# Conditioning weights in a ring of their own: whole visits, loaded one visit ahead

## The chip, the cores and the metric

The kernel runs on one core of one Trainium2 chip. The metric is the device time of one execution, in microseconds. Names used below: PE is the matrix engine (TensorE), PEld its weight loads, DVE the vector engine, ACT the scalar engine, POOL the third elementwise engine (GpSimd), SP the engine that issues the loads from HBM.

## The reference

One layer of a hybrid decoder, for 256 prompt tokens and 8 x 4 sample tokens (288 rows in all), model width 2048, all weights float32. What matters here:

```
mod = silu(c) @ w_ada + b_ada                  # nine conditioning rows, 2048 -> 6 x 2048
sh1, sc1, g1, sh2, sc2, g2 = split(mod, 6)     # "parts" 0 .. 5
h    = rmsnorm(x, norm1) * (1 + sc1) + sh1
proj = h @ w_in                                # pooled inputs, z gate, conv inputs, dt
mix  = concat(pool_mixer(...), ssd_mixer(...)) @ w_out
x    = x + g1 * mix
h2   = rmsnorm(x, norm2) * (1 + sc2) + sh2
up   = h2 @ w_up;  act = silu(causal_conv(gate)) * val
x    = x + g2 * (act @ w_down)
y    = rmsnorm(x, norm_f)
```

## The kernel before

All activations lie transposed: a tile holds 128 features by 288 rows. Every large product is done with three multiplications of a float32 value split in two (`mm3`, lines 302 to 304: weight high by input high, weight high by input low, weight low by input high). A weight block of 128 x 1024 (512 KB) is loaded into a *raw* slot, ACT casts it to the high half (line 288, `whi`), DVE subtracts to get the low half (line 290, `wlo`), and after that the raw slot is free. Eight PE products of 128 x 128 by three can be made from one block; one output tile of a 2048-long product takes two blocks and 48 matmuls.

The order of the work on PE is: the input projection in seven blocks (`xbc`), in the last of which all 28 tiles run over the last quarter of the input; then eight more tiles of it (`uz`), between which the state-space mixer (`ssd_group`, convolutions, pooling) runs; then the output projection, 16 tiles (`out`); then the second norm, the up projection (`upk`, `gate`, `val`) and the down projection.

The conditioning product `mod` has few rows, so for it the weights are the moving operand: parts 0 and 1 are needed first and are done during the early blocks. Parts 2, 3, 4 and 5 are done by `ada_part_units`: 16 steps over the 2048 inputs, each with two raw blocks (`adap`, 512 KB each) and four matmuls of 512 columns, which use a quarter of the array each (`tile_position`) and run side by side. A step's four matmuls are eight records in the trace. After the 16 steps the sum is copied (`asb`), transposed (`adat`) and added to the bias by DVE (line 419). Between two `yield`s lie AY = 2 steps, that is four blocks and 16 records: this is called a visit. Parts 2, 3 and 4 (the first gate, the second norm's shift and scale) are a chain `adas`, pulled at rates (RA1, RA2, TA, ADA_OUT) through the last `xbc` block, the `uz` tiles and the output projection, and part 5 (`adag2`) later.

```
adas = chain(*(ada_part_units(p, AY) for p in (2, 3, 4)))
...
pull(adas, RA1 / AY)          # each of the 28 tiles of the last xbc block
...
pull(adas, RA2 / AY)          # each eighth of a uz tile
...
pull(adas, TA / AY)           # once, before the output projection
...
pull(adas, (1 + (m >= 14 - ADA_OUT)) / AY)   # after each out tile
```

A scheduler places the instructions of each engine by its own estimate and may part the matmuls of one visit. Raw blocks of all kinds take turns in one ring of slots (class `_W`): 8 in the pool `w1`, 8 more in `w0` until the last `xbc` block, and one in `w2` from the sixth `out` tile on; `whi` and `wlo` have two slots in `w1` and two in `w2`. All these loads, those of the states (`h0`) and of `x` are issued by SP in one order; a load whose slot is not yet free holds up every load behind it.

Of the kernel before, what the change touches and what calls it, by code (L numbers as in the profile page):

```python
# [36 lines left out]
ET = XT + len(UEARLY) + 3 * ZEARLY  # L37
EPS = 1e-6
WU = (14, 2, 2, 2, 6)
RAW0, RAW1, RAW2 = 8, 8, 1  # L40
SPLIT0, SPLIT1, SPLIT2 = 1, 2, 2
YK = 2
AQ = (4, 4, 4, 4, 4, 4)
# [5 lines left out]
TP = 0.4  # L49
TV, TL = 2.0, 2.8  # L50
GB = 4
AY = 2

RA1, RA2, RB1, RB2, RB3 = 0.5, 0.4, 1.0, 1.0, 1.0
TA, ADA_OUT = 4, 4
TK = 4
GA = (2, 3)
XM = (0, 2, 5, 9)
# [105 lines left out]
def kernel(ctx: ExitStack, tc, ins, outs):  # L164
# [98 lines left out]

    wp = [None]

    def load(key):
        off, cols = S.items[key]
        t = wp[0].tile([P, RAWC], F32, tag="raw", name="raw_" + "_".join(map(str, key)))
        nc.sync.dma_start(t[:, :cols], wflat[off:off + P * cols].rearrange("(p n) -> p n", p=P))
        return t  # L270

# [3 lines left out]

    def top_up():

        while queue and nloads[0] - min((n for n, _ in ahead.values()), default=nloads[0]) < RAW0 + RAW1:
            key = queue.popleft()
            ahead[key] = (nloads[0], load(key))  # L280
            nloads[0] += 1
# [69 lines left out]
    def ada_group_units(gi):  # L351
# [49 lines left out]
            nc.vector.tensor_tensor(o, src, b.unsqueeze(3).to_broadcast([P, 2, nj // 2, NC9]), ALU.add)  # L401
        ada_scale(0, 1, early[:, V_N1:V_N1 + KT], k0, gk)

    def ada_part_units(part, ay=1):
        ps = pa.tile([P, 512], F32, tag="ada", name=f"adap{part}")
        for k in range(KT):
            raws = [load(("adap", part, k, h)) for h in range(2)]
            for h in range(2):
                ada_mm(ps, raws[h], k, 0, 512, range(2 * h, 2 * h + 2))
            if k % ay == ay - 1:  # L410
                yield
        asb = ada_sb(ps, 512, f"p{part}")
        yield
        pt = ada_tr(asb, 512, f"p{part}")
        for i in range(4):
            o = ada[:, part].rearrange("p (j i) c -> p j i c", j=4)[:, :, i, :]
            b = bada[:, part].rearrange("p (j i) -> p j i", j=4)[:, :, i]
            src = pt[:, i * P:(i + 1) * P].rearrange("p (j c) -> p j c", j=4)[:, :, 0:NC9]
            nc.vector.tensor_tensor(o, src, b.unsqueeze(2).to_broadcast([P, 4, NC9]), ALU.add)
        if part == 4:  # L420
            ada_scale(1, 4, vec[:, V_N2:V_N2 + KT], 0, KT)
        yield

    def samp(ap):
        return ap.rearrange("p (b l) -> p b l", b=NB)
# [30 lines left out]
    class _W:  # L456


        def __init__(self):
            self.slots = {"raw": [], "whi": [], "wlo": []}  # L460
            self.i = {"raw": 0, "whi": 0, "wlo": 0}

        def add(self, pool, nraw, nsp):
            for tag, n in (("raw", nraw), ("whi", nsp), ("wlo", nsp)):
                m = len(self.slots[tag])
                if m:
                    r = self.i[tag] % m
                    self.slots[tag] = self.slots[tag][r:] + self.slots[tag][:r]
                    self.i[tag] = 0
                self.slots[tag] += [(pool, n)] * n  # L470

        def drop(self, pool):
            for tag, sl in self.slots.items():
                r = self.i[tag] % len(sl)
                self.slots[tag] = [x for x in sl[r:] + sl[:r] if x[0] is not pool]
                self.i[tag] = 0

        def tile(self, shape, dt, tag, name):
            pool, n = self.slots[tag][self.i[tag] % len(self.slots[tag])]
            self.i[tag] += 1  # L480
            return pool.tile(shape, dt, tag=tag, name=name, bufs=n)

    wp[0] = _W()
    wp[0].add(ctx.enter_context(tc.tile_pool(name="w1", bufs=1, side="right")), RAW1, SPLIT1)
    mx_ctx = ExitStack()
    mx = mx_ctx.enter_context(tc.tile_pool(name="mx", bufs=1))
    xa = []
# [10 lines left out]
    w0_ctx = ExitStack()  # L498
    w0 = w0_ctx.enter_context(tc.tile_pool(name="w0", bufs=1))
    shift(w0, 32)  # L500
    wp[0].add(w0, RAW0, SPLIT0)
    sx = [None]

    cvp = [mx.tile([P, 5, CW], F32, tag="cvp", name=f"cvp{g}", bufs=4) for g in range(4)]
# [159 lines left out]
    def drain(gen):  # L664
        for _ in gen:
            pass
# [246 lines left out]
    def chain(*gens):  # L913
        for gn in gens:
            yield from gn

    adas = chain(*(ada_part_units(p, AY) for p in (2, 3, 4)))
    with in_order(*(e.engine for e in (nc.tensor, nc.scalar, nc.vector))):
        nc.scalar.activation(warm, sc_c[:, 0, 0:1], AF.Sqrt, scale=0.0)
        warm_pe(WU[0])  # L920
# [75 lines left out]
    def pull(gn, rate):  # L996

        credit[id(gn)] = credit.get(id(gn), 0.0) + rate
        while credit[id(gn)] >= 1:
            credit[id(gn)] -= 1  # L1000
            next(gn, None)

    nloads[0] = len(first) + KT // 4
    for bi in range(len(BLOCKS)):
        last = bi + 1 == len(BLOCKS)
        top_up()
        if last:

            wp[0].drop(w0)
            w0_ctx.close()  # L1010
            sx[0] = mx_ctx.enter_context(tc.tile_pool(name="sx", bufs=1, reuse_waits="tile"))
            raw = load(("dt",))[:, :KT * NH].rearrange("p (k h) -> p k h", h=NH)
            wdt = wp[0].tile([P, RAWC], F32R, tag="whi", name="whi_dt")
            with tc.high_priority():
                nc.gpsimd.memset(wdt.bitcast(F32), 0.0)
                both = wdt[:, :DTW * KT].rearrange("p (k c) -> p k c", c=DTW)
                nc.scalar.copy(both[:, :, 0:NH], raw)
                nc.vector.tensor_tensor(both[:, :, 32:32 + NH], raw, both[:, :, 0:NH].bitcast(F32), ALU.subtract)
            ps = pm.tile([P, 512], F32, tag="mm", name="mm_dt")
            for k in range(KT):  # L1020
                w = wdt[:, DTW * k:DTW * k + P]
                nc.tensor.matmul(ps[:, :N], w, xhi[0][k], start=k == 0, stop=False)
                nc.tensor.matmul(ps[:, :N], w, xlo[0][k], start=False, stop=k == KT - 1)
            late_states()
            dt_stage(ps)
        elif bi == 4:
            nc.sync.dma_start(vec, ins["vec"])
        elif bi == 5:
            late_loads()
        for i, m in enumerate(xbc_units(bi)):  # L1030
            if not last:
                top_up()
                if bi == 0 and i in (3, 7, 13):
                    ci = {3: 2, 7: 3, 13: 4}[i]
                    ready["xbc", 0, ci] = split(fetch(("xbc", 0, ci)), 0, len(_xbc_chunks(0)[ci][1]) * P,
                                                f"xbc0_{ci}", pin=True)
                if i in VIS[bi]:
                    next(nxt)
                    top_up()
            else:  # L1040
                pull(back, 0.5 if m < 20 else RB1) if m >= 9 else None
                pull(adas, RA1 / AY)

    late = {}
    n = 0
# [1 line left out]
    for m in list(range(4 + 3 * ZEARLY, 16)) + ULATE:  # L1047
        for _ in uz_units(m):
            n += 1
            for gn in late.values():  # L1050
                pull(gn, 0.5)
            pull(adas, RA2 / AY)
            pull(back, RB2 if n <= zlast else RB3)
            if n == zlast:
                drain(back)
                back = chain(ssd3, y_norm())
        if m < 4:
            late[m] = pool_units(m)
            next(late[m])
    pull(adas, TA / AY)  # L1060
    for h, (_, n) in enumerate(_halves(KT)):
        ready[("out", 0, h)] = split(load(("out", 0, h)), 0, n * P, f"out_0_{h}")
    for gn in late.values():
# [68 lines left out]
    for m in range(16):  # L1132
        if m in XM:
            sl = slice(4 * XM.index(m), 4 * XM.index(m) + 4)
            nc.sync.dma_start(x[:, sl, :], ins["x"][:, sl, :])
        if m == 5:
            wp[0].add(w2, RAW2, SPLIT2)
        for i, ps in enumerate(project_units(("out", m), KT, order=MIXK)):
            if m == KT - 1 and i == 5:
                all_but_last("ssum2")  # L1140
        residual(ps, 2, m)
        squares(m, "a")
        pull(adas, (1 + (m >= 14 - ADA_OUT)) / AY)
        if m == 13:
            drain(adas)


    adag2 = ada_part_units(5)
    for k in range(2):
        ready[("upk", k)] = split(load(("upk", k)), 0, 2 * FK * P, f"upk{k}")  # L1150
# [282 lines left out]
```

## Time and profile before

| | us |
|---|---|
| median of 3 runs | 1358.78 |
| lowest, highest | 1358.45, 1361.12 |
| the profiled execution's own time | 1359.14 |
| its span, first to last instruction | 1357.2 |
| PE busy | 1340.9 |
| DVE, ACT, POOL busy | 808.8, 580.3, 223.8 |
| moved by DMA | 323.18 MB |

The profile page gives busy time by engine, then 40 slices of the span, the DMA queues, the chain of work that ended last, and groups of instructions. The other views are asked of the same trace: the waits of an engine, the chain in order of time, a timeline of one engine, and sums over windows of time. A PE record's end is modelled, so the distance from one start to the next is the better price of a matmul.

### The profile page before, as it was taken

The page shows a single profiled execution, that of the slowest core. Times are in us where ns is not written, and L with a number is a line of the kernel's source. Part 1 is how long each engine was busy: PE and PEld are TensorE (multiplying, and loading weights), DVE is VectorE, ACT ScalarE, POOL GpSimd, SP SyncE. Part 2 cuts the span into 40 slices and gives each one's busy share as a digit, 9 for nine tenths or more (in the row PEclk, how much of TensorE's full clock was granted, in tenths as well). Part 3 has the DMA queues.
Part 4 walks back from the last instruction along what each step waited for, and adds up shares of the span by engine and source line. Part 5 has one row for each costly group of instructions (what it writes and reads, how often), then busy time and mean ns, then how long its engine had stood idle before and what let it go on. Part 6 is the DMA issues. An engine that isn't in the chain of part 4 may idle for free.

```text
span 1357.2 us, 26159 instructions
## 1 busy us (share of the span) xinstructions
PE 1340.9 (99%) x10517; PEld 1249.0 (92%) x10517; DVE 808.8 (60%) x1348; ACT 580.3 (43%) x911; POOL 223.8 (16%) x435
## 2 busy tenths in 40 slices
PE   9999999999999999999999999999999999999997
PEld 8889997776779889999999999999999999999997
DVE  5675568778564348645565455656554556566553
ACT  5343244577543335534443334443433334444452
POOL 0000012123121213111211001311220011132221
PEclk9999999999999999999999999999999999999999
DMA  9999768878878878787555555655555555566541
GB/s 371 405 408 365 257 245 320 341 263 296 301 278 321 323 263 261 244 288 272 184 184 184 162 180 183 201 190 184 176 186 167 186 188 192 187 205 191 181 120 70
DMA packets 97481, 323.18 MB, mean 238 GB/s; under 512 B 10768, under 2 KB 19920, under 8 KB 97360
## 3 DMA queue, kind: packets, MB, share of 16 engines
q1 hardware_dynamic: 93600, 310.79, 66.1%
q0 software_dynamic: 3184, 9.69, 2.0%
q8 instruction: 82, 1.34, 0.4%
q10 hardware_dynamic: 576, 1.03, 0.2%
q14 instruction: 39, 0.32, 0.1%
HBM read 309.78 MB, written 10.39 MB: 236 GB/s over the span
## 4 chain that ended last, share of the span: by engine, by line
PE 74%; DVE 1%; issue 0%; POOL 0%; ACT 0%; DVEq 0%; POOLq 0%
PE mm_down L303 7%; PE mm_down L302 7%; PE mm_down L304 7%; PE mm_val L303 6%; PE mm_gate L303 6%; PE mm_gate L302 6%; PE mm_val L304 6%; PE mm_gate L304 6%; PE mm_val L302 6%; PE adap L331 3%; PE mm_out L302 3%; PE mm_out L303 3%; PE mm_out L304 3%; PE mm_up L303 1%; PE mm_up L302 1%; PE mm_up L304 1%
## 5 line engine op out<-in xcount | busy, mean ns | idle before, releaser
L303 PE MATMUL mm_down<-al,whi_down 128*128 128x288 f32 x688 | 202.5, 294 | 0.0
L302 PE MATMUL mm_down<-ah,whi_down 128*128 128x288 f32 x688 | 202.4, 294 | 0.0
L304 PE MATMUL mm_down<-ah,wlo_down 128*128 128x288 f32 x688 | 202.0, 294 | 0.0
L303 PE MATMUL mm_gate<-h2l,whi_gate 128*128 128x288 f32 x640 | 188.8, 295 | 0.0
L303 PE MATMUL mm_val<-h2l,whi_val 128*128 128x288 f32 x640 | 188.8, 295 | 0.0
L304 PE MATMUL mm_val<-h2h,wlo_val 128*128 128x288 f32 x640 | 188.7, 295 | 0.0
L304 PE MATMUL mm_gate<-h2h,wlo_gate 128*128 128x288 f32 x640 | 188.6, 295 | 0.0
L302 PE MATMUL mm_gate<-h2h,whi_gate 128*128 128x288 f32 x640 | 188.5, 294 | 0.0
L302 PE MATMUL mm_val<-h2h,whi_val 128*128 128x288 f32 x640 | 187.7, 293 | 0.0
L290 DVE TENSOR_TENSOR wlo_gate<-raw_gate,whi_gate 128x1024 fp32r<-128x1024 f32 x80 | 98.2, 1229 | 136.5 <-ACT whi_gate L288 136.3
L290 DVE TENSOR_TENSOR wlo_down<-raw_down,whi_down 128x1024 fp32r<-128x1024 f32 x96 | 107.5, 1120 | 116.9 <-ACT whi_down L288 116.9
L288 ACT CAST whi_down<-raw_down 128x1024 fp32r<-128x1024 f32 x96 | 92.5, 964 | 167.0 <-PE mm_down L303 117.8
L288 ACT CAST whi_gate<-raw_gate 128x1024 fp32r<-128x1024 f32 x80 | 84.2, 1054 | 159.7 <-PE mm_gate L303 66.9
L288 ACT CAST whi_val<-raw_val 128x1024 fp32r<-128x1024 f32 x80 | 84.2, 1053 | 120.8 <-issue 101.6
L302 PE MATMUL xbc<-h1h,whi_xbc 128*128 128x288 f32 x448 | 133.4, 301 | 0.8 <-ACT h1h L452 0.7
L303 PE MATMUL xbc<-h1l,whi_xbc 128*128 128x288 f32 x448 | 132.0, 296 | 0.0
L304 PE MATMUL xbc<-h1h,wlo_xbc 128*128 128x288 f32 x448 | 130.0, 295 | 0.0
L302 PEld LDWEIGHTS mm_down<-ah,whi_down 128*128 128x128 f32 x688 | 129.2, 188 | 0.0
L303 PEld LDWEIGHTS mm_down<-al,whi_down 128*128 128x128 f32 x688 | 129.1, 188 | 0.0
L304 PEld LDWEIGHTS mm_down<-ah,wlo_down 128*128 128x128 f32 x688 | 129.0, 188 | 0.0
L302 PEld LDWEIGHTS mm_gate<-h2h,whi_gate 128*128 128x128 f32 x640 | 120.3, 188 | 5.0 <-ACT ah L1198 3.4
L302 PEld LDWEIGHTS mm_val<-h2h,whi_val 128*128 128x128 f32 x640 | 120.3, 188 | 0.0
(325 smaller groups left out, 2983.4 us busy)
## 6 DMA issues: line engine op xcount, KB each, us to landing
raw_adap<-wflat SPq DMA_DIRECT2D x128, 512.0 KB, 6.1
raw_gate<-wflat SPq DMA_DIRECT2D x80, 512.0 KB, 3.5
raw_val<-wflat SPq DMA_DIRECT2D x80, 512.0 KB, 3.9
raw_ada<-wflat SPq DMA_DIRECT2D x64, 512.0 KB, 9.6
raw_xbc<-wflat SPq DMA_DIRECT2D x50, 512.0 KB, 9.1
raw_down<-wflat SPq DMA_DIRECT2D x48, 512.0 KB, 3.6
raw_out<-wflat SPq DMA_DIRECT2D x32, 512.0 KB, 7.4
raw_down<-wflat SPq DMA_DIRECT2D x32, 384.0 KB, 3.1
```

The costliest lines, as they stand in the source:

```text
L288: yield nc.scalar.copy(hi[:, :n], raw[:, a:a + n])
L290: yield hi, lo, nc.vector.tensor_tensor(lo[:, :n], raw[:, a:a + n], hi[:, :n].bitcast(F32), ALU.subtract)
L302: nc.tensor.matmul(ps, whi[:, w], bh, start=first, stop=False)
L303: nc.tensor.matmul(ps, whi[:, w], bl, start=False, stop=False)
L304: nc.tensor.matmul(ps, wlo[:, w], bh, start=False, stop=last)
L331: nc.tensor.matmul(ps[32 * j:32 * j + 32, :nb], sc_c[:, k, :], raw[:, c:c + nb], start=(k == 0), stop=(k == KT - 1), tile_position=(0, 32 ...
```

## The change

Parts 2 and 3 are now done by a new generator, `ada_visits`, in visits of two steps (AK = 2); part 4 in four visits of four steps (AK2 = 4) after the output tiles 2, 5, 8 and 11. A visit's loads are issued one visit ahead, right behind the matmuls of the visit before. Its matmuls take the blocks in reverse order, so that the first one waits for the last load, and are tied to each other (high priority, program order), so that the scheduler keeps them together. The blocks have a ring of their own, `rawa`: four of the eight slots of `w1` go over to it when the last `xbc` block begins, and four more in `w2` join it at the first output tile (RAW2 = 4); at the end of the output projection all eight return to the common ring, which then has 12 slots where it had 9. From the last `xbc` block to the end of the output projection the ring of all other weights has four slots. The two `whi` and `wlo` slots of `w2` join at the first output tile instead of the sixth. VA spreads the 16 visits of parts 2 and 3: five in the last `xbc` block, nine in `uz`, the rest drained before the output projection.

```diff
-RAW0, RAW1, RAW2 = 8, 8, 1
+RAW0, RAW1, RAWA, RAW2 = 8, 4, 4, 4
-AY = 2
-RA1, RA2, RB1, RB2, RB3 = 0.5, 0.4, 1.0, 1.0, 1.0
-TA, ADA_OUT = 4, 4
+VA = (5, 9, 2)
+AK, AK2, AOUT = 2, 4, (2, 5, 8, 11)
...
+    def ada_visits(parts, step):
+        plan = [(part, k0) for part in parts for k0 in range(0, KT, step)]
+        def chunks(v):
+            part, k0 = plan[v]
+            return [(k, h, load(("adap", part, k, h), "rawa")) for k in range(k0, k0 + step) for h in range(2)]
+        ahead, end = chunks(0), None
+        yield
+        for v, (part, k0) in enumerate(plan):
+            if end:
+                ada_end(*end)
+                end = None
+            if k0 == 0:
+                ps = pa.tile([P, 512], F32, tag="ada", name=f"adap{part}")
+            n = 0
+            for k, h, raw in ahead[::-1]:
+                for j in (2 * h, 2 * h + 1):
+                    with tc.high_priority() if n else nullcontext():
+                        i = nc.tensor.matmul(ps[32 * j:32 * j + 32, :], sc_c[:, k, :],
+                                             raw[:, 512 * (j % 2):512 * (j % 2) + 512], start=k == step - 1,
+                                             stop=k == KT - step, tile_position=(0, 32 * j))
+                    tc.keep_in_program_order(i)
+                    n += 1
+            if v + 1 < len(plan):
+                ahead = chunks(v + 1)
+            if k0 + step == KT:
+                end = part, ada_sb(ps, 512, f"p{part}")
+            yield
+        ada_end(*end)
+        yield
...
-    adas = chain(*(ada_part_units(p, AY) for p in (2, 3, 4)))
+    adas = ada_visits((2, 3), AK)
...
             wp[0].drop(w0)
+            wp[0].move("rawa", "raw", "rawa")
...
+            next(adas)
             dt_stage(ps)
...
-                pull(adas, RA1 / AY)
+                pull(adas, VA[0] / 28)
...
-            pull(adas, RA2 / AY)
+            pull(adas, VA[1] / 64)
...
-    pull(adas, TA / AY)
+    drain(adas)
...
-        if m == 5:
-            wp[0].add(w2, RAW2, SPLIT2)
+        if m == 0:
+            for tag, n in (("rawa", RAW2), ("whi", SPLIT2), ("wlo", SPLIT2)):
+                wp[0].add(w2, tag, tag, n)
+            adas = ada_visits((4,), AK2)
+            next(adas)
...
-        pull(adas, (1 + (m >= 14 - ADA_OUT)) / AY)
+        if m in AOUT:
+            next(adas)
         if m == 13:
             drain(adas)
+    wp[0].move("rawa", "rawa", "raw")
     adag2 = ada_part_units(5)
```

More of the change, by code (lines that the diff above doesn't have):

```diff
@@ L51 @@
 GB = 4
-AY = 2
-RA1, RA2, RB1, RB2, RB3 = 0.5, 0.4, 1.0, 1.0, 1.0
-TA, ADA_OUT = 4, 4
+VA = (5, 9, 2)
+AK, AK2, AOUT = 2, 4, (2, 5, 8, 11)
+RB1, RB2, RB3 = 1.0, 1.0, 1.0
 TK = 4
@@ L264, with load @@
     wp = [None]
-    def load(key):
+    def load(key, ring="raw"):
         off, cols = S.items[key]
-        t = wp[0].tile([P, RAWC], F32, tag="raw", name="raw_" + "_".join(map(str, key)))
+        t = wp[0].tile([P, RAWC], F32, tag=ring, name="raw_" + "_".join(map(str, key)))
         nc.sync.dma_start(t[:, :cols], wflat[off:off + P * cols].rearrange("(p n) -> p n", p=P))
@@ L276, in top_up @@
     def top_up():
-        while queue and nloads[0] - min((n for n, _ in ahead.values()), default=nloads[0]) < RAW0 + RAW1:
+        while queue and nloads[0] - min((n for n, _ in ahead.values()), default=nloads[0]) < RAW0 + RAW1 + RAWA:
             key = queue.popleft()
@@ L413, in ada_part_units, with ada_end @@
         yield
+        ada_end(part, asb)
+        yield
+    def ada_end(part, asb):
         pt = ada_tr(asb, 512, f"p{part}")
@@ L421, in ada_part_units @@
             ada_scale(1, 4, vec[:, V_N2:V_N2 + KT], 0, KT)
-        yield
     def samp(ap):
@@ L459, in __init__, with turn, add, move @@
         def __init__(self):
[L460 to L470, printed above, removed]
+            self.slots = {"raw": [], "rawa": [], "whi": [], "wlo": []}
+            self.i = dict.fromkeys(self.slots, 0)
+        def turn(self, ring):
+            sl = self.slots[ring]
+            r = self.i[ring] % len(sl) if sl else 0
+            self.slots[ring], self.i[ring] = sl[r:] + sl[:r], 0
+        def add(self, pool, ring, tag, n):
+            self.turn(ring)
+            self.slots[ring] += [(pool, tag, n)] * n
+        def move(self, tag, a, b):
+            self.turn(a)
+            self.turn(b)
+            self.slots[b] += [x for x in self.slots[a] if x[1] == tag]
+            self.slots[a] = [x for x in self.slots[a] if x[1] != tag]
         def drop(self, pool):
[L473 to L476, printed above, removed]
+            for ring in self.slots:
+                self.turn(ring)
+                self.slots[ring] = [x for x in self.slots[ring] if x[0] is not pool]
         def tile(self, shape, dt, tag, name):
-            pool, n = self.slots[tag][self.i[tag] % len(self.slots[tag])]
-            self.i[tag] += 1
+            pool, tag, n = self.slots[tag][self.ix(tag)]
             return pool.tile(shape, dt, tag=tag, name=name, bufs=n)
+        def ix(self, ring):
+            self.i[ring] += 1
+            return (self.i[ring] - 1) % len(self.slots[ring])
     wp[0] = _W()
-    wp[0].add(ctx.enter_context(tc.tile_pool(name="w1", bufs=1, side="right")), RAW1, SPLIT1)
+    w1 = ctx.enter_context(tc.tile_pool(name="w1", bufs=1, side="right"))
+    for ring, tag, n in (("raw", "raw", RAW1), ("raw", "rawa", RAWA), ("whi", "whi", SPLIT1), ("wlo", "wlo", SPLIT1)):
+        wp[0].add(w1, ring, tag, n)
     mx_ctx = ExitStack()
@@ L500 @@
     shift(w0, 32)
-    wp[0].add(w0, RAW0, SPLIT0)
+    for tag, n in (("raw", RAW0), ("whi", SPLIT0), ("wlo", SPLIT0)):
+        wp[0].add(w0, tag, tag, n)
     sx = [None]
```

## The prediction

> **What bounds the kernel now.** I read the page first, then what PE waited for.
>
> ```profile
> span 1357.2 us, 26159 instructions
> PE 1340.9 (99%) x10517; PEld 1249.0 (92%) x10517; DVE 808.8 (60%) x1348; ACT 580.3 (43%) x911; POOL 223.8 (16%) x435
> ```
>
> ```profile
> PE mm_out L303 <- DVE mixl L1082: 2.0, 1, 2.0
> PE ysum L240 <- POOL ssq L839: 1.2, 1, 1.2
> PE cse L800 <- DVE ada L419: 1.0, 1, 1.0
> ```
>
> PE is busy for 99% of the span. So time can come from two places only: PE work that is not needed, and PE waits, of which the second view (waiter, releaser, total, times, longest) has 4.2 us in the part that changes. Everything else is hidden as long as data is there when PE comes to it. The page has nothing on pieces of visits, so next I read the timeline of PE round a whole visit, the chain round a broken one, and the sum over all of them.
>
> ```profile
> 403.67 0.29 PE L304 MATMUL mm_out<-mixh,wlo_out 128*128 128x288 f32 x1
> 403.90 1.92 PE L331 MATMUL adap<-raw_adap,sc_c 128*32 128x512 f32 x16
> 405.75 0.40 PE L302 MATMUL mm_out<-mixh,whi_out 128*128 128x288 f32 x1
> 405.99 0.29 PE L303 MATMUL mm_out<-mixl,whi_out 128*128 128x288 f32 x1
> ```
>
> ```profile
> 358.56 0.98 PE adap L331 x2
> ...
> 360.50 1.85 PE adap L331 x14
> ```
>
> ```profile
> 196.18:475.00 278.82, 54.71 (x384) 10.70 (x384) 1.18 (x2) 0.99 0.83 306
> ```
>
> A whole visit takes PE from 403.90 to 405.75, 1.85 us. The matmul before it and the one behind it take 0.23 and 0.24 us to the next start; the plain step is 0.134 (405.75 to 418.64 below, 96 matmuls in 12.89). So a visit between full-width matmuls costs another 0.2. In the second view a visit was parted: one matmul (two records) takes 0.98 alone, because its three neighbours do not run beside it, and the rest still takes 1.85: 2.83 instead of 1.85. The third row sums all of parts 2 to 4 (384 records, 24 visits): 54.71 us of PE.
>
> **What the change removes on PE.** 24 whole visits would be busy for 24 x 1.92 = 46.1, so 8.6 is spent on pieces; 0.9 of it lies in half clock, as the piece that starts at 383.40 in the chain shown below, and belongs to the next part, which leaves 7.7. I count 33 runs in the timeline, nine more than visits; a run's record overlaps the next by 0.07 (1.92 against 1.85), so 7.1 is real. In the order in which the changed kernel was built, every visit of parts 2 to 4 stands whole: 16 of 16 records and four of 32.
>
> ```profile
> 501.72 0.76 PE ssum L240 x6
> 502.48 0.97 PE adap L331 x2
> 503.46 0.79 PE pbrstd L253 x6
> 504.24 2.71 PE adap L331 x22
> ```
>
> 24 records (two are missing) take 2.71, so 8 more cost 0.86 and a visit of 32 takes 3.57, 0.13 less than two of 16; four of them 0.5. Between full-width matmuls there are 19 runs now and 11 in the new order: 8 x 0.2 = 1.6. Sum: 7.1 + 0.5 + 1.6 = **9.2 us less**. PE itself hides nothing of it, since it is the bound; what can take it back is a wait.
>
> The 1.0 us wait for DVE's bias addition goes as well: PE stood at a small matmul (`cse`) whose PSUM buffer still held a transposed conditioning sum; in the new order a whole visit, 1.85 us, lies between that transpose and the next `cse`. **1.0 less** (at worst nothing).
>
> **What it moves into a wait: the way into the output projection.** Here PE waits for the gated norm's chain, and this is where the moved visits were filling in.
>
> ```profile
> 364.79 1.42 POOL ssq L839
> ...
> 366.26 0.83 PE ysum L240 x6
> ...
> 370.01 1.13 PE pbrstdy L253 x6
> ...
> 376.11 1.18 DVE wlo_out L290
> ...
> 379.74 0.44 DVE mixl L1082
> ...
> 380.22 0.40 PE mm_out L303
> ...
> 383.40 0.99 PE adap L331
> ```
>
> ```profile
> 364.63:368.05 3.42, 2.22 (x18) 1.99 (x17) 3.39 (x10) 1.91 (x5) 1.42 (x1) 1.00 0.89 307
> 368.05:371.46 3.41, 3.41 (x16) 3.37 (x15) 0.02 (x1) 0.30 (x1) 0.00 (x0) 0.50 0.99 392
> 378.29:381.70 3.41, 1.48 (x8) 1.29 (x9) 3.36 (x13) 2.88 (x8) 0.00 (x0) 1.00 0.98 362
> 381.70:385.11 3.41, 3.41 (x10) 1.54 (x8) 3.41 (x8) 0.44 (x1) 0.47 (x1) 0.50 1.02 418
> ```
>
> The windows (length, busy PE, PEld, DVE, ACT, POOL, then granted clock, DMA share, GB/s) show that each wait here is paid again: after 1.2 and 1.9 us of idle PE in a stretch of 3.41 us the clock is 0.50 for the next 3.41, about 1.7 us lost. The Trainium skill ("TensorE: Matmul & The Clock Gate", section "What's actually happening") grants half the clock after an idle window of about 3.4 us and asks for no gaps above that length; here 1.2 us sufficed, so the trace is harsher than the page.
>
> Now: 1.2 + 1.7 + 2.0 + 1.7 and 0.5 of small change, 7.1 us lost between the last `y` and the end of the third output tile. Changed: between that `y` and `ysum` stand 15 matmuls (2.1 us) instead of 19 and most of a visit; the chain from y to ssq takes about 2.6 by my estimate when ACT is free (1.42 at most for ssq, and three steps of the size of mixl, 0.44), so a wait of 0.5 and no half clock. From `pbrstdy` to the first `mixl` I take 8.6: now 380.2 - 370.0 = 10.2, less one `wlo_out` (1.2), which is done earlier in the new order, and less 0.4 at full clock. PE has only `pbrstdy`, a pool product, three matmuls and one visit in that time, 3.5 us: a wait of 5.1, and half clock behind it, 1.7. Together 7.3 against 7.1. I take **0.2 more** (the visits gone as filler equal the work that is gone; between -2 and +3).
>
> **The third output tile's second half.** This is the new wait.
>
> ```profile
> DMA to landing us min/median/max: 3.3/6.1/13.2
> ```
>
> ```profile
> 405.75:418.64 12.89, 12.89 (x101) 1.00 0.96 371
> 473.11:485.90 12.79, 12.79 (x101) 1.00 1.00 382
> ```
>
> ```profile
> 374.94 1.92 PE L331 MATMUL adap<-raw_adap,sc_c 128*32 128x512 f32 x16
> ```
>
> ```profile
> 375.70 1.05 ACT L288 CAST whi_out<-raw_out 128x1024 fp32r<-128x1024 f32 x1
> ```
>
> ```profile
> 376.03 0.80 SPq L269 DMA_DIRECT2D raw_adap<-wflat  x2
> ```
>
> SP's queue is in order: behind a load that waits for its slot, all that follows waits too. A load takes 3.3 us or more to land, and in a full stretch (the two windows of PE alone above) 382 GB/s are 1.37 us for 512 KB; I use 3.6 for the first and 1.35 for each further one. In the new order SP has, behind the last visit of part 3: two blocks of `adap`, one more, a piece of `x`, another block, a piece of `x`, and only then the second half of output tile 2. The first waits until that visit has given up its first slot, 1.1 us after its start (in the profile SP's next loads follow the visit at 374.94 at 376.03). The seventh lands 1.1 + 3.6 + 6 x 1.35 = 12.8 us after the visit's start, and the cast (1.05) and subtraction (1.18 above) follow. PE has the rest of the visit, 52 matmuls at 0.134 and about 1.2 of small products: 10.1 us. So the first matmul waits 12.8 + 1.1 - 10.1 = 3.8 and the third another 1.0, and 4.8 idle bring half clock for one window: 4.8 + 1.7 = **6.5 more** (between nothing, if SP gets the blocks in earlier, and 9). Who waits behind it: every later output tile, and nothing else.
>
> **The rest of the output projection.** A long visit needs eight blocks: 3.6 + 8 x 1.35 = 14.4 us, and behind them come the next tile's two. The ring of four holds two tiles, 12.9 us; the first blocks are asked for some 2.5 us before the visit ends, as its slots come free. That leaves about 0.5 short at the sixth tile, nothing at the others, where the new order has more of `out` ahead of the eight: **0.5 more** (0 to 7, see the rivals). In `uz` and `xbc` four blocks need 1.1 + 3.6 + 3 x 1.35 = 8.8 us from one visit's start to the next; by the new order the shortest distance is 9.8, so nothing.
>
> **The second norm.** Today one visit lies before `ssum`, a piece of 0.97 behind it and 22 records behind `pbrstd`. In the new order the third column sum stands behind a lone matmul: ssum in two parts with 0.97 between, then eight records (0.99), `pbrstd`, 14 records (1.85), and the modulated input comes about 3.1 after `pbrstd`'s start. 1.85 + 0.55 + 0.97 + 0.4 + 0.99 + 3.1 = 7.9 against 504.24 + 2.71 - (501.72 - 1.85) = 7.1 now: **0.8 more**. In the up and down projections PE waits for nothing now, and twelve slots instead of nine can win nothing there.
>
> **Sum**: -9.2 - 1.0 + 0.2 + 6.5 + 0.5 + 0.8 = -2.2 us against the profiled execution's own 1359.14 (its span 1357.2 and 1.9 round it), that is 1356.9. That execution was 0.4 above the median of the runs, 1358.78; from the median I get 1356.6 and take **1356.7**. No change can be told from one within 0.2%, 1356.1 to 1361.5.
>
> **Rivals.** *The third tile does not wait* (faster). If SP's loads get in earlier, or the 1.0 and half clock fall away, 6.5 goes: 1350.2. For it: SP's order was set by an estimate, and DMA had 0.83 of its time taken from 196 to 475, so there is room. Against it: the slots' order, which no speed of DMA changes.
>
> *Four slots are too few* (slower). If a block takes over 1.35 us, the eight blocks of a long visit and the next tile's (9 x 1.35 + 3.3 = 15.5) outlast two tiles and the lead of 2.5 (15.4). At 1.5 (the median landing of 6.1 shows how far the queue is filled) each of two gaps is 1.7 us late and pays 1.7 at half clock: 6.8 more, 1363.5. For it: 371 GB/s in a normal stretch. Against it: PEclk 1.00 and no wait in the stretch from 405 to 500 today, with the same bytes.
>
> *The clock falls only after a whole idle window*, as the page named above has it. Then 1.7 behind the third tile's wait is not paid: 1355.0. The windows above speak against it, the wait of 1.0 us at `cse`, which cost no clock, a little for it.
>
> **Chances.** Forecast (1354 to 1360) 0.45; third tile free 0.20; four slots too few 0.27; clock 0.08. Faster by over 0.2%: 0.20 + 0.08 + 0.17 of the forecast's 0.45 (what lies below 1356.1) = 0.45; within: 0.28 + 0.05 of the slower case that ends below 1361.5 = 0.33; slower 0.22. The range leaves out the lower half of the faster case and the upper part of the slower one: 1350 to 1364; the likeliest case's own is 1354 to 1360.
>
> **What would show it.** Right: PE time of `adap` up to the end of the output projection about 46 (16 x 1.92 + 4 x 3.64), no run of two records; a wait of `mm_out` for `mixl` near 5 and one for `whi_out` near 4; the clock at 0.50 twice. Wrong: `whi_out` released by DMA at several tiles (four slots), no wait at the third tile, a broken visit, or waits of `adap` for its own blocks.

## The result: 6 us slower, and the profile after

The changed kernel takes 1364.93 us (median of 5 runs, 1364.44 to 1366.04) against 1358.78 before (5 runs, 1358.04 to 1361.12): a ratio of 1.0044, with a 95% interval of 1.003 to 1.0058. The forecast was 1356.7 (1350 to 1364): the wrong side of no change, by 8 us. The profiled execution took 1366.04, with a span of 1364.3, 7.1 more than before.

The page of the changed kernel, first lines:

```profile
span 1364.3 us, 26129 instructions
PE 1336.8 (98%) x10517; PEld 1251.2 (92%) x10517; DVE 813.7 (60%) x1348; ACT 580.4 (43%) x911; POOL 219.7 (16%) x435
```

PE is busy for 4.1 us less, in a span that is 7.1 longer: the work went, and 11 us of idling came. The visits' own PE time in the changed kernel, to be held against the 54.71 of before:

```profile
199.56:480.00 280.44, 46.22 (x384) 10.58 (x384) 0.97 0.83 303
```

It is 8.5 less. With 13 runs of records fewer (33 to 20, at an overlap of 0.07) that is 7.6 of real time, and 7.6 is what the forecast had for pieces and long visits. What PE waited for in the changed kernel (waiter, releaser, total, times, longest):

```profile
PE mm_out L302 <- ACT whi_out L288: 5.2, 2, 4.3
PE mm_out L303 <- DVE mixl L1132: 4.8, 1, 4.8
PE adap L424 <- DMA raw_adap<-wflat: 1.2, 2, 0.6
PE mm_out L304 <- DVE wlo_out L290: 1.1, 2, 0.7
...
PE y L864 <- ACT ec L854: 0.7, 1, 0.7
PE cse L848 <- DVE yo L834: 0.7, 1, 0.7
PE pool L935 <- DVE pout L930: 0.6, 1, 0.6
PE ysum L240 <- POOL ssq L887: 0.4, 1, 0.4
```

Before there were 4.2 us of waits in this part. Here are first three waits of the forecast: `mixl` (4.8, forecast 5.1), the third output tile (4.3 and 0.4, forecast 3.8 and 1.0) and `ysum` (0.4, forecast 0.5). Then come a second wait for `whi_out` at the sixth output tile (0.9, with 0.7 for its low half; forecast 0.5) and a row of waits of 0.5 to 0.7 in the `uz` part, which the forecast did not have. Two of these are a visit waiting for its own blocks (`adap`, 1.2 in all). The clock, in stretches of 3.41 us, the steps in which it changed in these traces (busy PE, PEld, DVE, ACT, POOL, then PEclk, DMA share, GB/s):

```profile
368.25:371.66 3.41, 1.34 (x5) 1.34 (x6) 3.41 (x13) 3.22 (x7) 0.13 (x1) 0.50 1.02 372
371.66:375.08 3.42, 3.42 (x19) 1.83 (x22) 3.42 (x8) 1.38 (x4) 0.00 (x0) 0.50 0.90 367
395.56:398.97 3.41, 0.85 (x2) 0.50 (x2) 1.11 (x1) 1.89 (x2) 0.79 (x1) 0.50 1.03 410
398.97:402.39 3.42, 3.25 (x13) 3.25 (x14) 3.23 (x4) 2.29 (x3) 0.00 (x0) 0.50 0.82 268
422.87:426.28 3.41, 3.41 (x16) 3.41 (x15) 3.41 (x3) 1.81 (x2) 0.16 (x1) 0.50 0.72 191
```

A full-width matmul follows the one before it after 0.24 us at clock 0.50 and after 0.134 at 1.00, so nearly half of the busy time at 0.50 is lost; taken as half it is 2.4, 2.05 and 1.7, together 6.1 us. Before it was 3.4 in two windows. Last, the two places where `whi_out` was late: SP's loads, and the chain back from PE.

```profile
375.65 10.32 SPq L269 DMA_DIRECT2D raw_adap<-wflat  x8
...
387.76 11.69 SPq L269 DMA_DIRECT2D raw_out<-wflat  x5
```

```profile
387.76 9.01 DMA raw_out<-wflat
396.79 1.05 ACT whi_out L288
```

```profile
404.79 4.97 SPq L269 DMA_DIRECT2D raw_adap<-wflat  x8
409.86 16.88 SPq L269 DMA_DIRECT2D raw_out<-wflat  x8
```

```profile
397.86 5.08 DVE L290 TENSOR_TENSOR wlo_out<-raw_out,whi_out 128x1024 fp32r<-128x1024 f32 x4 [3.89 <-ACT whi_out L288]
```

At the third tile the output load goes out at 387.76. Since the output load before it, at 360.65, SP has issued sixteen loads of `adap` and two pieces of `x`; the last four `adap`, from 384.69 on, waited for the last visit's slots. The output load lands 9.0 later, the cast takes 1.05, and PE starts at 397.88. At the sixth tile the eight blocks of one long visit go out at 404.79, the tile's first half behind them at 409.86, and it takes 10.1 to land. From 399.9 to 404.79 SP stood for the visit's first slot. In that time three of the four output slots came free: the four subtractions of the last view end at 399.1, 400.4, 401.7 and 402.9, and only the first slot was taken at once. So here too the output load stood behind the visit's loads in the queue, and not only for want of a slot.

### The profile page after: what moved, and what is told of

Its sections match the earlier page's. It is cut to its first block, busy times and chain, and to the rows that moved or that the text cites. A ratio compares the mean times of both kernels' runs of the same rounds, so it can differ in the third digit from the quotient of the medians.

```text
span 1364.3 us, 26129 instructions
## 1 busy us (share of the span) xinstructions
PE 1336.8 (98%) x10517; PEld 1251.2 (92%) x10517; DVE 813.7 (60%) x1348; ACT 580.4 (43%) x911; POOL 219.7 (16%) x435
## 3 DMA queue, kind: packets, MB, share of 16 engines
q8 instruction: 82, 1.34, 0.4%
## 4 chain that ended last, share of the span: by engine, by line
PE 92%; DMA 4%; DVE 2%; ACT 1%; issue 0%; SPq 0%; POOL 0%; DVEq 0%; POOLq 0%; ACTq 0%
PE mm_down L303 7%; PE mm_down L302 7%; PE mm_down L304 7%; PE mm_val L303 6%; PE mm_gate L303 6%; PE mm_gate L302 6%; PE mm_val L304 6%; PE mm_gate L304 6%; PE mm_val L302 6%; PE xbc L302 5%; PE xbc L303 4%; PE xbc L304 4%; PE adap L424 3%; PE mm_out L304 2%; PE mm_out L303 2%; PE mm_out L302 2%
```

## Experiments

Times are medians of 4 to 12 runs, and each ratio is to the kernel before on the same chip, which took 1358.4 to 1358.9 in all of them.

**Part 4 asked for later, in long visits.**

```
-AK, AK2, AOUT = 2, 4, (2, 5, 8, 11)
+AK, AK2, AOUT = 2, 4, (4, 7, 10, 13)
...
                 wp[0].add(w2, tag, tag, n)
+        if m == 3:
             adas = ada_visits((4,), AK2)
             next(adas)
```

> The changed kernel, but part 4's first eight blocks are asked for ahead of output tile 3 instead of tile 0, and its four visits lie after tiles 4, 7, 10, 13. In the built order the second half of tile 2 is now loaded ahead of them. Theory Q (a place in SP's queue costs the time: the half tile behind part 4's first blocks): the wait at the third tile, 4.7 us, and its half clock, 2.0, go: 1364.9 - 6.7 = 1358.2. Rival S (four slots for the output weights are too few beside eight blocks of conditioning, wherever they stand): the wait comes back at tile 3, 3 to 5 us with half clock behind it: 1363 to 1366.

1361.21, ratio 1.0019 (1.0011 to 1.0028). The wait at the third tile is gone, one of 2.5 and 0.7 is there at the fourth (tile 3 of the code, where S had it), and the half clock behind it did not come in the profiled execution. That execution took 1358.70, 2.5 less than the median; what the others lose was not profiled. The median lies between Q and S: 3.7 of the 6.7 us that Q put on the place in the queue came back.

**Part 4 in short visits.**

```
-AK, AK2, AOUT = 2, 4, (2, 5, 8, 11)
+AK, AK2, AOUT = 2, 2, (2, 4, 5, 7, 8, 10, 11, 13)
```

> The changed kernel, but part 4 in eight visits of two steps (after tiles 2, 4, 5, 7, 8, 10, 11, 13) instead of four of four. In the built order the second half of tile 2 stands ahead of part 4's blocks here too, and no burst is longer than four blocks. Theory Q: the waits at the third tile (6.7 with half clock) and at the sixth (1.7 and 1.7) go, and four more switches and the shorter visits cost 1.3: 1364.9 - 10.1 + 1.3 = 1356.1. Rival S: a wait of 3 to 5 us comes back at tile 3, the sixth tile is free: 1361 to 1363.

1362.65, ratio 1.0027 (1.0018 to 1.0035). Waits of 1.0 and 0.7 stand at 399 (the fourth tile) and again at 447 (the tenth), the second with half clock. The first is in the rival's place, but 1.7 us and not 3 to 5; the second neither theory had. The rival's time, 1361 to 1363, is right in part by luck.

**Both.**

```
-AK, AK2, AOUT = 2, 4, (2, 5, 8, 11)
+AK, AK2, AOUT = 2, 2, (3, 4, 6, 7, 9, 10, 12, 13)
...
                 wp[0].add(w2, tag, tag, n)
+        if m == 2:
             adas = ada_visits((4,), AK2)
             next(adas)
```

> The changed kernel with both edits: part 4 in eight visits of two steps after tiles 3, 4, 6, 7, 9, 10, 12, 13, its first four blocks asked for ahead of tile 2. Theory Q: as with the short visits, 1356; the y-norm's wait of 4.8 and its half clock stay. Rival S: a wait of 3 to 5 at tile 3 or 4, 1361.

1361.01, ratio 1.0014 (1.0005 to 1.0022): the rival's number, but not its wait. In the profile 0.7 and 0.7 of waiting for output weights are left, at the sixth tile, without half clock. That execution is the fastest of the eleven (1357.84), so its trace doesn't show what the median still loses. By the medians, order and length of the loads gave back 4 us of the 10 that both waits had cost.

**The four new slots for the output weights.** This is the short-visit kernel, with one word changed.

```
         if m == 0:
-            for tag, n in (("rawa", RAW2), ("whi", SPLIT2), ("wlo", SPLIT2)):
+            for tag, n in (("raw", RAW2), ("whi", SPLIT2), ("wlo", SPLIT2)):
```

> The short visits of part 4 (1362.6), but the four new slots of the second pool go to the output weights at tile 0, not to the conditioning: eight for the weights, four for the visits. Theory S (four slots are too few for the output weights beside the conditioning): the waits of 1.7 us at 399 and at 447 and the half clock behind the second go: 1362.6 - 1.7 - 1.7 - 1.7 = 1357.5. Rival (the blocks come late by order and traffic, whatever the slots): 1361 to 1363.

1358.05, ratio 0.9996 (0.9987 to 1.0004), level with the kernel before. PE's longest waits with short visits, and then with the slots given to the output weights:

```profile
PE mm_out L303 <- DVE mixl L1132: 4.8, 1, 4.8
PE mm_out L302 <- ACT whi_out L288: 2.0, 2, 1.0
PE mm_out L304 <- DVE wlo_out L290: 1.5, 2, 0.7
```

```profile
PE mm_out L303 <- DVE mixl L1132: 4.8, 1, 4.8
PE warm L228 <- DVE ones L193: 1.1, 1, 1.1
```

No wait for an output weight is left in the profiled execution, with the same bytes and visits of the same length, and the time is theory S's (1357.5). The run doesn't show slots alone, though. The edit takes four slots from the visits as it gives them to the weights, and the order of the loads changes with it: where the short-visit kernel issues ten loads of `adap` in a row from 366.87 on, this one issues two of `out`, four of `adap` and two of `out`. From the changed kernel's 1364.93 this edit and the short visits give back 6.9 us. The waits of the `uz` part and at `mixl` are still there.

**Whole visits in the old ring.** The kernel before, with one edit.

```
-            for h in range(2):
-                ada_mm(ps, raws[h], k, 0, 512, range(2 * h, 2 * h + 2))
+            if part < 5:
+                todo += [(k, h, raws[h]) for h in range(2)]
+                if k % ay == ay - 1:
+                    n = 0
+                    for kk, h, raw in todo[::-1]:
+                        for j in (2 * h, 2 * h + 1):
+                            with tc.high_priority() if n else nullcontext():
+                                i = nc.tensor.matmul(...)
+                            tc.keep_in_program_order(i)
+                            n += 1
+                    todo = []
+            else: ...        # part 5 as before
```

> The kernel before, with one edit: the matmuls of a visit of parts 2, 3 and 4 are tied together and take their blocks in reverse, in the common ring, loaded as before. In the built order one visit is still parted (by the dt transposes), all others stand whole. Theory W (whole visits are worth what their pieces cost, 8 us less 1.0 for the parted one, and the ring is not needed for it): no new wait, 1358.8 - 6.5 = 1352. Rival R (a tied visit makes PE wait for its last block, which the pieces had covered): waits of adap for its loads of 4 us or more, 1357 to 1361.

1357.21, ratio 0.9986 (0.9977 to 0.9994): faster, but by 1.2 us and not 6.5. The visits' PE time, and the waits:

```profile
196.18:480.00 283.82, 48.45 (x384) 10.17 (x384) 0.99 0.85 315
```

```profile
PE mm_out L303 <- DVE mixl L1097: 3.2, 1, 3.2
PE ysum L240 <- POOL ssq L854: 1.2, 1, 1.2
PE warm L228 <- DVE ones L193: 1.1, 1, 1.1
PE cse L815 <- DVE ada L434: 0.8, 1, 0.8
```

6.3 us of PE time went (54.71 to 48.45), and some 2 of waiting came: 1.2 more for `mixl`, and several of 0.3 to 0.5. The list of PE's waits has none for a visit's blocks, so rival R's reason is not what happened. The profiled execution (1355.05) is the lowest of the eleven; what the others add was not profiled. Up to the column sums of the y-norm (`ysum`), visits alone and PE as a whole, first in the kernel before and then with whole visits:

```profile
196.18:366.26 170.08, 37.21 (x256) 7.29 (x256) 1.00 0.83 305
196.18:366.26 170.08, 167.38 (x1317) 1.00 0.83 305
```

```profile
196.18:363.43 167.25, 33.06 (x256) 6.84 (x256) 1.00 0.85 313
196.18:363.43 167.25, 164.30 (x1318) 1.00 0.85 313
```

The visits take 4.15 us less there, PE idles for 2.95 us instead of 2.70, and the sums start 2.8 us earlier. So in the common ring hardly any wait takes the place of the pieces up to here.

**Pieces in the new ring.** The missing one of the four combinations: the changed kernel with the matmuls untied and in the order of the loads.

```
-            for k, h, raw in ahead[::-1]:
+            for k, h, raw in ahead:
                 for j in (2 * h, 2 * h + 1):
-                    with tc.high_priority() if n else nullcontext():
-                        i = nc.tensor.matmul(..., start=k == step - 1, stop=k == KT - step, ...)
-                    tc.keep_in_program_order(i)
+                    nc.tensor.matmul(..., start=k == 0, stop=k == KT - 1, ...)
```

> The changed kernel with the matmuls of a visit untied and in the loads' order (own ring and loads one visit ahead as in the change); in the built order parts 2 and 3 stand in pieces again, put between the small products of the state-space groups, and 14 loads lie ahead of the second half of output tile 2 instead of six. Theory F (the pieces filled PE's waits): up to the column sums of the y-norm PE waits less than 2 us instead of 4.3, the visits cost 4 to 6 us more, and the sums start 1 to 3 us later than in the changed kernel. Rival (the waits are the ring's): 4 us of waits stay and the sums start 5 us later. In both the third tile waits longer than in the change, and the time is 1366 to 1372.

1374.33, ratio 1.0114 (1.0101 to 1.0128). The third tile waited less than in the changed kernel (2.7), not longer as expected. The loss is in the output projection all the same: the scheduler laid two visits there in four pieces each, 0.98 apiece (3.9 us instead of 1.85). Up to the up projection the visits take 14.0 us more than whole, and PE waits 7.8 less. What it was made for is the time up to the y-norm's column sums, which start at 361.03 here and at 358.61 in the changed kernel. Visits alone, and PE as a whole; in each pair the untied one comes first:

```profile
196.18:361.03 164.85, 32.88 (x208) 6.08 (x208) 1.00 0.77 275
```

```profile
196.18:358.61 162.43, 25.01 (x208) 5.42 (x208) 1.00 0.79 287
```

```profile
196.18:361.03 164.85, 164.57 (x1268) 1.00 0.77 275
```

```profile
196.18:358.61 162.43, 158.13 (x1286) 1.00 0.79 287
```

The same 208 records take 7.9 us less when whole. But PE idles for 0.3 us with pieces and for 4.3 with whole visits, so 4.0 of the 7.9 are taken back by waits. The sums start 2.4 us earlier, with 17 more `uz` matmuls done by then, some 2.3 us of work. Theory F's reason holds in this ring: the scheduler had put the pieces where PE else waits, for the state-space chain and for a visit's own blocks. Its sizes do not all: the pieces cost 7.9 and not 4 to 6, and the time lies above its 1366 to 1372.

**Parts 2 and 3 in the common ring, still loaded one visit ahead.**

```
-RAW0, RAW1, RAWA, RAW2 = 8, 4, 4, 4
+RAW0, RAW1, RAWA, RAW2 = 8, 8, 0, 4
-            return [(k, h, load(("adap", part, k, h), "rawa")) ...]
+            return [(k, h, load(("adap", part, k, h), "rawa" if part == 4 else "raw")) ...]
+AK, AK2, AOUT = 2, 2, (2, 4, 5, 7, 8, 10, 11, 13)
```

> The changed kernel with parts 2 and 3 in the common ring of eight slots (no ring of their own until the output projection), and part 4 in eight visits of two steps with four slots of its own in the second pool. In the built order three whole visits stand one behind another between the last uz matmul and the first output matmul. Theory P (a private ring of four holds just one visit, so none is in reserve when PE waits for the y-norm): the wait for mixl falls from 4.8 to 1 or less with no half clock, and the tiles 2 and 5 do not wait: 1364.9 - 10.1 - 3.8 - 2.4 + 1.3 = 1350. Rival: the three visits need twelve blocks and the ring has eight, so PE waits for their loads instead, 3 to 5 us: 1355 to 1357.

1397.13, ratio 1.0282 (1.0268 to 1.0296). Both expectations missed; the waits show why:

```profile
PE adap L424 <- DMA raw_adap<-wflat: 8.8, 3, 6.6
PE xbc L302 <- ACT whi_xbc L288: 7.9, 3, 3.9
PE mm_uz L302 <- ACT whi_uz L288: 7.3, 10, 1.7
```

The wait for `mixl` is gone, as P had it, but PE waits 6.6 us for a visit's loads in that place, as the rival had it, and for the weights of `xbc` and `uz` long before. My reading is that a visit's blocks, which sit one visit long in a common slot, keep out those weights; no run shows that by itself.

**More slots for whole visits.** The whole-visit kernel with `RAW2 = 4` and the second pool joined at tile 0.

> The kernel before with whole visits (as in the run with the old ring, 1357.2), and four common slots with the two cast slots of the second pool from output tile 0 on instead of one from tile 5. Theory: slots were not what the output projection lacked there (its only wait besides the norm's was 0.3 us), so the time stays: 1356.5 to 1357.5. Rival: earlier loads bring a visit into the norm's wait of 3.25, 1 to 2 us less: 1355.5.

1357.29, ratio 0.9988 (0.9979 to 0.9997). Nothing, as expected: with eight common slots the output projection lacked none.

**Keeping PE busy in the wait.** Ten matmuls of ones were put ahead of the first one that needs `mixl`.

```
+    wps = aux("warm2")
+    with tc.high_priority():
+        for _ in range(10):
+            nc.tensor.matmul(wps[:, :P], ones, xhi[0][MIXK[0]][:, 0:P].bitcast(F32), start=True, stop=True)
...             # and the first matmul that reads mixl is tied behind them
```

> The kernel before with whole visits (1357.2), and ten matmuls of 128x128 of ones that nothing reads between the first matmul of the output projection and the one that waits for mixl, so PE is busy in 2.4 of the 3.25 us of that wait. Theory C (the half clock behind a wait follows from idle PE in the window before): the clock stays at 1.00 behind it and the wait's end does not move: 1357.2 - 1.7 = 1355.5. Rival: the half clock does not depend on it, or the ten matmuls put off the work behind them: 1357 to 1358.

1359.68, ratio 1.0003 (0.9995 to 1.0012), above both expectations. It decides nothing on the clock: a pool product ahead of the ten waited 3.6 us for DVE, so they ran after the wait, and the kernel is 2.5 us slower than with whole visits alone. It showed that PE waits there for another of DVE's results as well, `pout` in the place of `mixl`.

**mixl first.** Where DVE is queued, the first group's `mixl` stand behind work that PE does not need yet.

```
+            with tc.high_priority() if g < 1 else nullcontext():   # g < 4: all twelve
                 nc.scalar.activation(xhi[0][k], zy[g][:, t, :], AF.Identity, scale=gv)
                 nc.vector.scalar_tensor_tensor(out=xlo[0][k], ...)
```

With whole visits in the old ring, first group:

> The kernel before with whole visits (1357.2), and the three high halves and mixl of the first normed group at high priority, so DVE makes the first two mixl ahead of the second weight subtraction, the convolution pieces and the bias addition that stood before them (some 3.5 us of DVE). Theory D (what PE waits for on its way into the output projection is DVE's queue, not the norm): the wait of 3.25 falls to 0.5 or less and its half clock (1.7) goes: 1357.2 - 2.8 - 1.7 = 1352.7. Rival E (PE then waits for the later mixl or for the second weight half, in pieces, as DVE's work in that stretch is the same): 1356 to 1358.

1357.87, ratio 0.9995 (0.9987 to 1.0004): rival E. The wait of 3.2 became 0.9 and 1.6, and the half clock stayed.

All twelve:

> The same with all twelve mixl at high priority: the pieces of the pooled inputs come behind them. Theory D: as with the first group, 1352 to 1353. Rival E: the pooled operands, needed last, become late, and PE waits for them at the end of the second tile: 1356 to 1359.

**1355.56, ratio 0.9976 (0.9968 to 0.9985): the fastest here, faster than both kernels.**

```profile
PE mm_out L304 <- DVE wlo_out L290: 1.4, 1, 1.4
PE ysum L240 <- POOL ssq L854: 1.2, 1, 1.2
PE mm_out L303 <- DVE mixl L1098: 1.1, 2, 0.9
```

```profile
364.00:374.00 10.00, 9.12 (x70) 7.41 (x70) 7.79 (x15) 6.36 (x12) 2.90 (x2) 1.00 0.45 181
374.00:384.00 10.00, 7.33 (x46) 6.42 (x47) 10.00 (x26) 4.95 (x12) 2.67 (x6) 1.00 1.02 371
384.00:394.00 10.00, 10.00 (x75) 8.12 (x74) 5.17 (x11) 3.01 (x5) 0.82 (x3) 1.00 0.92 320
```

The time lies between D's and E's. DVE is busy for all of 374 to 384, and PE still loses 2.7 there, but in three pieces, and the clock stays at 1.00. D's size was too large: the wait is parted, not taken away. The gain over whole visits alone is one of the medians, 1.65 us; the profiled execution (1355.13) is no faster than the one profiled there (1355.05), which had the half clock.

In the changed kernel, first group; and with late short visits:

> The changed kernel with the first group's high halves and mixl at high priority. In the built order DVE makes mixl behind two of the three zy and one weight subtraction: 4.4 us after rstdy instead of 7.0. Theory D: the wait of 4.8 falls to 2.2, its half clock from 2.4 to 1.7 lost: 1364.9 - 2.6 - 0.7 = 1361.6; the third tile's wait (it hangs on SP's queue) stays. Rival E: 1364 to 1366.

> The changed kernel with part 4 in eight short visits, its first blocks asked for ahead of tile 2 (1361.0), and mixl of the first group at high priority. Theory D and Q together: 1361.0 - 3.3 = 1357.7, level with the kernel before, as the visits that would fill the rest of the norm's wait are still on their way in the ring of four. Rival E: 1361.

1367.35, ratio 1.0064 (1.0052 to 1.0077), and 1358.79, ratio 0.9999 (0.999 to 1.0008). In both the wait of 4.8 parts in two (1.95 and 1.75, 1.96 and 2.16). The first lies above both its expectations, as it loses more elsewhere: its built order of loads differs, and the third tile waits 5.0 and the visits 3.7. The second gains 2.2 of the 3.3 forecast for it by the medians.

**Slots for the output weights and all mixl first.**

> The kernel of e12 with all twelve mixl at high priority. Theories S and D together: 1357.5 less 2 to 4 us for the wait on the way into the output projection: 1354 to 1356, level with the whole visits in the old ring with mixl first (1355.6). Rival: the private ring's next visit still lands late, so PE waits in that place: 1357 to 1359.

1365.23, ratio 1.0047 (1.0034 to 1.006). Both missed. `mixl` is down to 2.0, but SP's queue stands for 8 us behind the slots of a visit, as it does in the kernel without the edit, and one output load was out ahead of that, where it had been two. First the kernel without, then the one with the edit:

```profile
366.37 0.84 SPq L269 DMA_DIRECT2D raw_out<-wflat  x2
374.53 1.91 SPq L269 DMA_DIRECT2D raw_adap<-wflat  x4
```

```profile
366.24 0.33 SPq L269 DMA_DIRECT2D raw_out<-wflat  x1
375.06 1.76 SPq L269 DMA_DIRECT2D raw_adap<-wflat  x4
```

The output weights come late twice (1.8 and 1.4, each with 0.7 for the low half and a window of half clock), at the fifth and the eleventh tile and with eight slots of their own. That the one load fewer ahead is the reason is my reading. In none of the eight versions with the own ring was the time clearly below that of the kernel before.

## Why the forecast was wrong

Up to the start of the up projection the changed kernel is 7.0 us later. Summed from one PE start to the next, from 196 us on, the forecast's steps stand so:

| step | forecast | measured |
|---|---|---|
| visits whole, long visits | -7.6 | -7.5 (57.2 to 49.7) |
| switching | -1.6 | +0.7 (all other PE work at full clock) |
| PE waits | +6.2 (-1.0 + 1.9 + 4.8 + 0.5) | +11.1 (4.7 to 15.8) |
| lost to half clock | 0 | +2.7 (3.4 to 6.1) |
| second norm | +0.8 | +0.7 (part of the rows above) |
| sum | -2.2 | +7.0 |

The two edits in one, visits whole and a ring of their own, give four combinations. Visits, waits and half clock are summed as above, from the profiled executions:

| | median time | visits | waits | half clock |
|---|---|---|---|---|
| common ring, pieces (before) | 1358.78 | 57.2 | 4.7 | 3.4 |
| common ring, whole | 1357.21 | 52.1 | 6.5 | 1.7 |
| own ring, pieces | 1374.33 | 63.7 | 8.0 | 3.4 |
| own ring, whole (the change) | 1364.93 | 49.7 | 15.8 | 6.1 |

Whole visits gain in either ring: 1.2 us in the common one (against 1358.43 on the same chip) and 9.4 in the own one. The own ring, with its four slots for all other weights and its loads one visit ahead, loses in either case: 7.7 with whole visits and 15.6 with pieces. The forecast added the two up, 9.2 less for whole visits and 6.5 + 0.5 more for the loads. They do not add up: where the ring costs about what it had, whole visits gain 1.2, and where they gain 9.4, the ring costs 15.6.

- **Right:** what a visit costs whole or parted; the wait for `mixl`; the third tile (4.7 of waiting and 2.05 of clock, 6.8, forecast 6.5), its reason and its place; the split `ssum`; 46.22 us of visits where about 46 was named as the sign (its working gives 45.3, and 0.9 of the measured lies in half clock).
- **The step that failed is "PE itself hides nothing of it".** It took all cost of the pieces for waste, because PE had hardly a wait, and left a wait as the only thing that could take it back, with none in `uz`. In the own ring whole visits idle PE for 4.3 us up to the column sums and pieces for 0.3 (the untied run), so 4.0 of 7.9 were hidden. In the common ring it was next to nothing up to there (2.70 to 2.95), and 1.8 us over the whole stretch. So the pieces covered waits that the own ring brings; whether its order of visits or that of its loads makes them was not tried apart. The forecast also took the one wait left in `uz` (1.0 at `cse`) as a gain: 0.2 of it stayed, and new waits of 0.5 to 0.7 stand beside it.
- **A visit's own blocks** were taken to be in time in `uz`, at 8.8 us for four blocks against a shortest distance of 9.8. PE waited for them twice, 1.2 us in all, at visits that start 10.7 and 12.0 us after the one before: another term put at nothing.
- **Switching** did fall beside the visits: what the steps of full-width matmuls next to a visit cost above 0.134 is 4.8 before and 3.0 after, summed. But the same sum for matmuls next to a wait rose from 0.5 to 2.0, and of the small products of the state-space groups `cse` went from 3.7 to 4.6 and `y` from 13.7 to 14.0, while `s` fell from 5.7 to 5.1.
- **The sixth tile** was the mis-sized term: 0.5, and it measured 0.93 + 0.73 of waiting and 1.7 of clock, 3.4. The nine loads took 15.2 us from the first issue to the last landing where the forecast had 14.4, and it left out the low half and the clock. The rival "four slots are too few" came nearest in time, 1363.5, at a chance of 0.27, and that is luck in part. It had two such gaps and one came; its condition, over 1.35 us a block, was not met (the nine landings lie 1.34 apart); its own figures give 1.4 us a gap and not 1.7. The run with eight slots for the output weights has no such wait, but it changes the order of the loads too, and the last run waits twice with the same eight slots. So too few slots and the place in the queue are not parted here. What spoke against the rival, no wait in that stretch before with the same bytes, was seen with eight or nine common slots.
- **The clock** was taken at one window a wait. Behind `mixl` and at the third tile it was two. The rival by which only a wholly idle window costs the clock fell again: a window with 2.2 us of busy PE was followed by half clock (last section).

## What to carry to other kernels

When PE is 99% busy, ask of each small piece of work what would run in its place: a trace that shows few waits may show them filled, not absent, and how much is filled depends on the order of the rest (4.0 us in one ring here, 0.25 in the other). A private ring takes slots from the neighbours and puts its waiting loads ahead of theirs in one queue, so count slots and the order of the loads for both sides. And what a wait costs is the wait and the clock behind it: with all twelve `mixl` first, a wait of 3.2 us fell into three pieces and no half clock followed in the profiled execution.

## What was not expected of the hardware

The same idle time brought half clock in one execution and not in another. In the whole-visit kernel, and in the one with the first group's `mixl` first, PE was busy for 2.23 and 2.22 us of a window:

```profile
360.41:363.83 3.42, 2.23 (x18) 2.00 (x16) 2.49 (x5) 3.02 (x5) 1.42 (x1) 1.00 0.95 367
363.83:367.24 3.41, 3.41 (x28) 3.36 (x28) 1.37 (x8) 0.53 (x2) 0.00 (x0) 1.00 0.95 383
```

```profile
364.28:367.69 3.41, 2.22 (x18) 2.08 (x17) 3.11 (x10) 1.62 (x3) 1.28 (x1) 1.00 0.95 336
367.69:371.11 3.42, 3.42 (x16) 3.19 (x14) 0.39 (x1) 0.82 (x2) 0.35 (x1) 0.50 0.64 260
```

With part 4 asked for later, two windows on end with 1.78 and 1.86 busy kept the full clock. Over all sixteen traces, from 25 us after the start to 30 us before the end, I counted the windows that began at full clock. All 23 in which PE was busy for at most 1.57 us were followed by half clock, 7 of the 31 with 1.65 to 2.32 were, and none with more. So idle time alone does not tell between 1.65 and 2.32, and a wait's price may differ by 1.7 us between two executions; what else counts stays open. The full clock with all twelve `mixl` first had a window of 2.25 in it, so chance may have had a part.
